# A layer with product-key experts: 170 gathered tokens, 1 MB weight loads, and output chunks held in PSUM

## The chip, the cores and the metric

One core of a Trainium2 chip runs the whole layer. The metric is the device time of one execution in microseconds (us); the time before is the median of three runs.

## The reference

The layer has an attention part (a latent attention and a stick-breaking attention, gated and merged) over 512 frames and 16 meta tokens, and then an expert part, which the change is about. Width D is 2048; there are 16,384 experts, each a row of `u` and a row of `v`. Each token picks 16 experts in each of 8 heads, so 128 experts with weights:

```
q = (xb @ w_q).reshape(PEER_BLOCK, PEER_HEADS, 2, PEER_HALF)
s = einsum('thcd,hcnd->thcn', q, sub_keys)
s1, i1 = top_k(s[:, :, 0], 16);  s2, i2 = top_k(s[:, :, 1], 16)
top_s, top_pos = top_k(all sums s1 + s2, 16);  idx = the pairs' expert numbers
g = softmax(top_s)
h = einsum('tkd,td->tk', u[idx], xb)
act = g * gelu(h)
out = einsum('tk,tkd->td', act, v[idx])
```

The residual is added and a final RMSNorm taken.

## The kernel before

**Two ways for the experts.** Tokens are split. The first `ND` = 352 are *dense*: every expert is computed for all of them by matmuls, and a matrix of gates that is zero outside a token's 128 experts picks what counts. The last 160 are *gathered*: only their chosen rows of `u` and `v` are loaded, by indirect DMAs that GpSimd (POOL) issues, and VectorE (DVE) multiplies and sums them. Of these, 128 tokens lie one to a partition, one expert of each per load (128 loads of 1 MB). The other `NB` = 32 have `RB` = 4 partitions each, so 32 loads serve them. That makes `NR` = 160 row loads of `u` and as many of `v`.

**Precision.** Each fp32 weight tile of 128 x 1024 is loaded (`wr`), rounded by ScalarE (ACT) into `wh`, and VectorE makes the remainder `wl` (line 208). The moving side is split the same way. `mm3` (lines 218 to 221) then issues three matmuls for each 128 x 128 block of weights. `wr` has four buffers of 0.5 MB; in stage V every fourth weight tile takes `wr`, `wh` and `wl` from a small pool of its own, which makes five. `wh` and `wl` have three buffers and that one.

**Stage U** (line 1171) loops over 128 blocks of 128 experts. Each block loads two half tiles of `ut`, runs 48 matmuls of 352 columns into one PSUM bank, takes Gelu into `hb` and writes it to `h_d` in DRAM. Between the halves it advances two generators, both by hand: `steps` (routing of the three dense tiles of 128 tokens, on VectorE) and `gate_steps` (one-hot matmuls at line 1033 that build the gates, two per token, written to `g_d`). The gathered rows are spread by `PACE`: a curve of rows done against block number. `OWN` says from which row on the buffers of the group loads are no longer lent to rows. `send` issues a row load and `row_step` works a row off on VectorE (lines 1126 and 1133).

**Stage V** (line 1242) loops over 32 groups of 512 experts. `hin` and `gin` bring a group's hidden values and gates in, `gated` multiplies them, `group_split` rounds them into `vah` and `val`. Eight weight tiles of `vb` (256 output columns each) follow, giving 16 output chunks of 128 features, each with 12 matmuls. `TURN` alternates the order of the tiles, so that the last three tiles of a group come first in the next and their six chunks stay in PSUM between the two (`held_ps`). Every other chunk is added to `acc` in SBUF after each group (line 1291). The residual `ht_d` is loaded in pieces in groups 3 to 18. In the last group the gathered tokens' sums are brought into place, `fin_add` squares and sums, and `fin_out` norms and writes.

**Order.** The language's scheduler orders each engine's instructions. Every queue is then worked off in that order: SP issues the weight, `hin` and `gin` loads, POOL the row loads, ACT the residual loads. The extra dependencies in the code (without a wait) keep the rows spread.

Of the kernel before, what the change touches and what calls it, by code (L numbers as in the profile page):

```python
# [37 lines left out]
NB = 32  # L38
RB = P // NB
ND = TA - NB  # L40
# [6 lines left out]
NG = NK // GRP  # L47
IN_SPLITS = (512, 512, 64, 1024, 1024, 1024, D, D)
# [59 lines left out]
def _layout(x, positions, meta_tokens, norm_mix_g, w_in, mla_q_norm_g, mla_w_uq, mla_kv_norm_g,  # L108
# [52 lines left out]
    ut = u.reshape(NK, NK, 2, 8, P).transpose(0, 2, 4, 3, 1).reshape(NK * 2, P, 1024)  # L161
    vb = v.reshape(NG, GRP, P, 8, 256).transpose(0, 3, 2, 1, 4).reshape(NG * 8, P, 1024)
# [20 lines left out]
def body(tc, nc, a, dbg=None):  # L183
# [10 lines left out]
    more = {"n": 0, "pool": None, "raw": False, "of": (4, (1,))}  # L194

    def wtile(src, eng=None, parts=False):
# [3 lines left out]
        raw = (w_ if more["raw"] else wp).tile([P, 1024], F32, name="wr", tag="wr",  # L200
                                               bufs=1 if extra and more["raw"] else 4)
        hi = w_.tile([P, 1024], F32R, name="wh", tag="wh")
        lo = w_.tile([P, 1024], F32R, name="wl", tag="wl")

        def load(s):
            SP.dma_start(raw[:, s], src[:, s])
            more["last"] = S.activation(hi[:, s], raw[:, s], AF.Copy)  # L207
            more["lo"] = (eng or V).tensor_sub(lo[:, s], raw[:, s], hi[:, s].bitcast(F32))  # L208

        if parts:  # L210
            return hi, lo, load
        load(slice(0, 1024))
        return hi, lo
# [36 lines left out]
    gwb_d = dp.tile([NB, P], F32, name="gwb_d")  # L250
    eob_d = dp.tile([NB, P], I32, name="eob_d")
# [3 lines left out]
    def rstd(out, ssq, n, dim, pool, tags=("rs_v", "rs_r", "rs_t")):  # L255
        w = n // (2 if n > 512 else 1)
        for c0 in range(0, n, w):
            ps = ps_tile()
            T.matmul(ps[:, :w], ones, ssq[:, c0:c0 + w], start=True, stop=True)
            v = pool.tile([P, 512], F32, name="rs_v", tag=tags[0])  # L260
            r0 = pool.tile([P, 512], F32, name="rs_r", tag=tags[1])
            t = pool.tile([P, 512], F32, name="rs_t", tag=tags[2])
# [518 lines left out]
    with tc.tile_pool(name="outp", bufs=2, side="right") as op:  # L781
        late = []

        def natural(m, gr):
            pt_ = ps_tile()
            for j, x_ in enumerate((xg, xgb)):
                T.transpose(pt_[:, j * P:(j + 1) * P], gr[:, j], ident)
                S.activation(x_[:, m * P:(m + 1) * P], pt_[:, j * P:(j + 1) * P], AF.Copy)

        for m in range(KC):  # L790
# [25 lines left out]
            V.tensor_scalar(gr[:, 1].rearrange("p (t r) -> p t r", r=RB),  # L816
# [15 lines left out]
    actb = rp.tile([P, NB], F32, name="actb")  # L832
    gwb = rp.tile([P, NB], F32, name="gwb")
    eob = rp.tile([P, NB], I32, name="eob")
# [20 lines left out]
    def spread_rows():  # L855
        b0 = ND - (NT - 1) * P
        SP.dma_start(eob_d, er[b0:])
        SP.dma_start(gwb_d, gw_all[b0:, NT - 1])
        SP.dma_start(eob, eob_d.rearrange("t (r k) -> (t r) k", r=RB))
        SP.dma_start(gwb, gwb_d.rearrange("t (r k) -> (t r) k", r=RB))  # L860

# [44 lines left out]
    with tc.tile_pool(name="score", bufs=2, side="left") as sp_, \  # L906
# [28 lines left out]
        for hc in range(16):  # L935
# [28 lines left out]
            if hc == 1:  # L964
                pt_ = ps_tile()
                rr = sp_.tile([P, 4, NK], F32, name="sc")[:, 0]
                V.tensor_copy(rr.rearrange("p (t r) -> p t r", r=RB), rh_[:, ND:TA, None].to_broadcast([P, NB, RB]))
                T.transpose(pt_[:, :P], rh_[:, TA:], ident)
                T.transpose(pt_[:, P:2 * P], rr, ident)
                V.tensor_copy(rcol, pt_[:, :1])  # L970
                V.tensor_copy(rcolb, pt_[:, P:P + 1])
            if hc:
                scores(*late.pop(0))
            if hc % 8 == 0:
                wr_ = wp.tile([P, 1024], F32, name="wr", tag="wr", bufs=4)
# [29 lines left out]
    def gates_of(ti):  # L1005
# [10 lines left out]
        for t0 in range(0, n + 4, 4):  # L1016
            if t0:
                p0 = t0 - 4
                oh_, wo_ = (spare[c][:, p0 // 4 % 2] for c in range(2))
                for t in range(4):  # L1020
# [3 lines left out]
            if t0 < n:  # L1024
                V.tensor_tensor(spare[0][:, t0 // 4 % 2], idx[:, :, t0:t0 + 4, None].to_broadcast([P, 2, 4, P]),
                                iota_b, ALU.is_equal)
            yield
            gate_out()
            if t0:
                ps = ps_tile()  # L1030
                for t in range(4):
                    for c in range(2):
                        T.matmul(ps[:, t * P:(t + 1) * P], oh_[:, 1, t], wo_[:, c, t], start=c == 0, stop=c == 1)
                banks.append((ps, ti * P + p0))
            yield

# [3 lines left out]
    def gate_out(hold=3):  # L1040

        for _ in range(min(2, len(banks))):
            if banks[0][1] % TB == 0 and len(banks) < hold:
                return
            ps, tok = banks.pop(0)
# [6 lines left out]
            for hf, half in enumerate(gb["now"]):  # L1052
                after_gelu(S.activation(half[:, :, o:o + 4].rearrange("p i t -> p t i"),
                                        ps.rearrange("p (t f i) -> p f t i", t=4, f=2)[:, hf], AF.Copy))
                if o + 4 == TB or tok + 4 == ND:
# [33 lines left out]
    NR = P + NB  # L1089
# [3 lines left out]
    NU = NR + 6  # L1093
    PACE = (2, 12, 123, NK - 0.5), (0, 7, 161, NU)
    OWN = 156
# [3 lines left out]
    def send():  # L1099
# [14 lines left out]
        idx = eo[:, k:k + 1] if k < P else eob[:, k - P:k - P + 1]  # L1114
        G.indirect_dma_start(out=row[:], out_offset=None, in_=a[src],  # L1115
# [4 lines left out]
    def row_step(mark, lead):  # L1120
# [3 lines left out]
        (src, k), row = todo[n], rows.pop(n)  # L1124
        if src == "u":
            ins = V.scalar_tensor_tensor(row, row, 1.0, xg if k < P else xgb, ALU.mult, ALU.mult,  # L1126
                                         accum_out=act[:, k:k + 1] if k < P else actb[:, k - P:k - P + 1])
        else:
            y, w = (yv, act[:, k:k + 1]) if k < P else (yvb, actb[:, k - P:k - P + 1])
            if k in (0, P):  # L1130
                ins = V.tensor_scalar(y, row, w, None, ALU.mult)
            else:
                ins = V.scalar_tensor_tensor(y, row, w, y, ALU.mult, ALU.add)  # L1133
# [5 lines left out]
        if src == "u" and k == NR - 1:  # L1139
            S.activation(actb, actb, AF.Gelu, scale=rcolb)  # L1140
            V.tensor_mul(actb, actb, gwb)
# [29 lines left out]
    for e in range(NK):  # L1171
# [7 lines left out]
        ps = ps_tile()  # L1179
        for hf in range(2):  # L1180
            wh, wl = wtile(a["ut"][2 * e + hf])
# [7 lines left out]
            for _ in range(1 + hf if e < 12 or e % 8 == 0 else hf):  # L1189
                next(steps, None)  # L1190
# [3 lines left out]
        if e == NK - 2:  # L1194
            gated(*held[0])
            ready = [vi.tile([P, D], F32R, name=x, tag=t)[:, :GRP * ND].rearrange("p (j t) -> p j t", t=ND)
                     for x, t in (("vah", "gin"), ("val", "hin"))]
            split(*ready, held.pop(0)[0])
# [10 lines left out]
    more["raw"], more["of"] = True, (4, (0,))  # L1209
# [3 lines left out]
    def group_split(i, eng):  # L1213
        ah, al = [vp.tile([P, GRP, ND], F32R, name=x) for x in ("vah", "val")]
        split(ah, al, held.pop(i)[0], eng)
        return ah, al
# [15 lines left out]
    def fin_out(t0, t1):  # L1232
        rstd(rf[:, t0:t1], ssf[:, t0:t1], t1 - t0, D, vp)
# [6 lines left out]
    TURN = ((0, 1, 2, 3, 4, 5, 6, 7), (5, 6, 7, 3, 4, 0, 1, 2))  # L1240
    held_ps, begun = {}, set()
    for i in range(NG):
        ah, al = ready
        for g in {0: (1,), 1: (2, 3)}.get(i, ()):
            group_in(g)
        if i == NG - 1:
            assert gs["done"] == len(todo)
            ln_exp(more["last"])
            ps = ps_tile()
            for c in range(KC):  # L1250
                T.matmul(ps[:, c * NB:(c + 1) * NB], yvb[:, c * P:(c + 1) * P], C("sel"), start=True, stop=True)  # L1251
            V.tensor_add(acc[:, :, ND:TA], acc[:, :, ND:TA], ps[:, :KC * NB].rearrange("p (c t) -> p c t", t=NB))
# [7 lines left out]

        for qi, q8 in enumerate(TURN[i % 2]):
            wh, wl = wtile(a["vb"][i * 8 + q8])
            if i + 1 < NG and qi == QM:
                gated(*held[i + 1])
            if qi == 0 and 0 <= i - 3 < KC:
                hres = vp.tile([P, ND], F32, name="hres", bufs=1)
                for dst, t in ((hres, slice(0, ND)), (acc[:, i - 3, ND:], slice(ND, SEQ))):
                    ld = S.dma_start(dst, ht_d[i - 3][:, t])
                    tc.add_manual_dep(ld.ins, more["last"].ins.name, NOSYNC, reason="keeps the loads spread")
            if qi == 6 and 0 <= i - 3 < KC:  # L1270
                V.tensor_add(acc[:, i - 3, :ND], acc[:, i - 3, :ND], hres)
            if i + 1 < NG and qi == QS:
                ready = group_split(i + 1, V)
                if i and i + 3 < NG:
                    group_in(i + 3)
            for dc in range(2):
                c = q8 * 2 + dc
                goes_on, stays = c in held_ps, i + 1 < NG and qi >= 5
                ps = held_ps.pop(c) if goes_on else ps_tile()
# [4 lines left out]
                if stays:  # L1284
                    held_ps[c] = ps
# [9 lines left out]
                if i == NG - 1:  # L1295
                    fin_add(c, 0, ND, qi + dc == 0)
                    if (qi, dc) == (2, 0):
                        fin_out(ND, SEQ)
# [20 lines left out]
```

## Time and profile before

| | |
|---|---|
| median of 3 runs | 3680.87 us (3677.76 to 3683.68) |
| the profiled execution | 3683.72 us, span 3681.5 us |
| TensorE busy | 3630.1 us, 99% |
| VectorE, ScalarE, GpSimd busy | 71%, 40%, 19% |
| moved by DMA | 868.28 MB |
| stage U, stage V | about 1569 to 2657 us, 2657 to 3664 us |

The profile's page gives the busy share of each engine over the span and in 40 equal slices (one digit, tenths). A window's row gives, for each engine, busy us and number of instructions, then the granted clock of TensorE, the share that the 16 DMA engines were busy, and GB/s. A group's row gives line, engine, operation, out<-in, count, busy us and mean ns, and the engine's idle time just before with what ended it. A wait's row has total us, times and the longest.

### The profile page before, as it was taken

What the parts mean: (1) busy time and instruction counts of PE and PEld (TensorE: products, weight loads), DVE (VectorE), ACT (ScalarE), POOL (GpSimd) and SP (SyncE); (2) the same over time, 40 slices, a digit from 0 to 9 for tenths busy, and PEclk for the clock granted to TensorE, in tenths of its full rate; (3) what the DMA queues carried; (4) which work ended last, traced back from release to release, by engine and by line L of the source; (5) the groups of instructions that cost most, each with busy time, mean ns of one, the idle gap of its engine ahead of it and who ended that gap; (6) DMA issues with size and microseconds to landing.
All of it is one profiled execution on the core that took longest, in us unless ns stands there. A gap on an engine that the chain in (4) does not pass through costs nothing. (4 is left out here: it accounts for less than half of the span.)

```text
span 3681.5 us, 53353 instructions
## 1 busy us (share of the span) xinstructions
PE 3630.1 (99%) x21159; PEld 3377.5 (92%) x21159; DVE 2623.8 (71%) x3499; ACT 1475.3 (40%) x2360; POOL 702.1 (19%) x499
## 2 busy tenths in 40 slices
PE   9999999999999999999999999999999999999997
PEld 8888888887788878899999999999999999999997
DVE  5533334335644567899979877777689999999896
ACT  4233233234533232235656666664333333333333
POOL 1000000000011221112222322332232322322220
PEclk9999999999999999999999999999999999999998
DMA  4322222221144442268898989999899999999982
GB/s 167 101 100 92 98 93 97 95 98 41 46 143 138 144 156 87 97 250 298 318 351 309 374 335 341 348 342 362 318 374 368 366 365 365 370 357 348 350 335 96
DMA packets 216538, 868.28 MB, mean 236 GB/s; under 512 B 24352, under 2 KB 49632, under 8 KB 175328
## 3 DMA queue, kind: packets, MB, share of 16 engines
q1 hardware_dynamic: 132896, 463.49, 35.4%
q0 software_dynamic: 53440, 361.52, 25.7%
q10 hardware_dynamic: 29952, 39.86, 3.0%
q8 instruction: 166, 2.72, 0.3%
q14 instruction: 84, 0.69, 0.1%
HBM read 801.83 MB, written 62.95 MB: 235 GB/s over the span
## 5 line engine op out<-in xcount | busy, mean ns | idle before, releaser
L207 ACT ACTIVATE wh<-wr 128x1024 fp32r<-128x1024 f32 (+1 forms) x756 | 789.1, 1054 | 1511.5 <-PE ps L221 1346.2
L208 DVE TENSOR_TENSOR wl<-wr,wh 128x1024 fp32r<-128x1024 f32 (+1 forms) x741 | 935.3, 1270 | 512.4 <-ACT wh L207 507.7
L219 PE MATMUL ps<-hgh,wl 128*128 128x352 f32 (+1 forms) x2304 | 773.2, 336 | 10.5 <-DVE wl L208 9.6
L221 PE MATMUL ps<-hgh,wh 128*128 128x352 f32 (+1 forms) x2304 | 768.3, 333 | 0.0
L220 PE MATMUL ps<-hgl,wh 128*128 128x352 f32 (+1 forms) x2304 | 765.1, 332 | 2.1 <-DVE hgl L225 2.0
L219 PE MATMUL ps<-vah,wl 128*128 128x352 f32 x2048 | 664.0, 324 | 4.1 <-DVE wl L208 3.9
L221 PE MATMUL ps<-vah,wh 128*128 128x352 f32 x2048 | 664.8, 325 | 0.0
L220 PE MATMUL ps<-val,wh 128*128 128x352 f32 x2048 | 661.0, 323 | 0.0
L219 PE MATMUL ps<-xh,wl 128*128 128x512 f32 (+1 forms) x1376 | 472.0, 343 | 6.0 <-ACT xh L312 6.0
L220 PE MATMUL ps<-xl,wh 128*128 128x512 f32 (+1 forms) x1376 | 470.1, 342 | 0.2 <-DVE xl L313 0.2
L221 PE MATMUL ps<-xh,wh 128*128 128x512 f32 (+1 forms) x1376 | 470.1, 342 | 0.0
L219 PEld LDWEIGHTS ps<-hgh,wl 128*128 128x128 f32 x2304 | 434.6, 189 | 25.0 <-DVE wl L208 11.9
L220 PEld LDWEIGHTS ps<-hgl,wh 128*128 128x128 f32 x2304 | 434.3, 189 | 14.5 <-DVE hgl L225 2.8
L221 PEld LDWEIGHTS ps<-hgh,wh 128*128 128x128 f32 x2304 | 433.5, 188 | 11.5 <-issue 0.2
L219 PEld LDWEIGHTS ps<-vah,wl 128*128 128x128 f32 x2048 | 386.2, 189 | 5.2 <-DVE wl L208 5.2
L221 PEld LDWEIGHTS ps<-vah,wh 128*128 128x128 f32 x2048 | 388.5, 190 | 0.0
L220 PEld LDWEIGHTS ps<-val,wh 128*128 128x128 f32 x2048 | 388.3, 190 | 0.0
L1115 POOL DMA_INDIRECT row<-v,eo x128 | 217.4, 1698 | 568.4 <-DVE xg L1133 522.7
L1133 DVE SCALAR_TENSOR_TENSOR xg<-row,act,xg 128x2048 f32<-128x2048 f32 x127 | 298.3, 2349 | 7.8 <-DMA row<-v,eo 7.8
L1115 POOL DMA_INDIRECT row<-u,eo x128 | 186.0, 1453 | 610.7 <-DVE row L1126 537.3
L219 PEld LDWEIGHTS ps<-xh,wl 128*128 128x128 f32 x1376 | 259.5, 189 | 37.8 <-ACT xh L312 6.4
L1126 DVE SCALAR_TENSOR_TENSOR row<-row,xg 128x2048 f32<-128x2048 f32 x128 | 292.5, 2285 | 0.5 <-DMA row<-u,eo 0.5
(453 smaller groups left out, 4744.8 us busy)
## 6 DMA issues: line engine op xcount, KB each, us to landing
wr<-ut SPq DMA_DIRECT2D x256, 512.0 KB, 6.3
wr<-vb SPq DMA_DIRECT2D x256, 512.0 KB, 6.7
wr<-front SPq DMA_DIRECT2D x238, 512.0 KB, 3.3
h_d<-hb ACTq DMA_DIRECT2D x128, 176.0 KB, 5.4
g_d<-gb POOLq DMA_DIRECT2D x44, 512.0 KB, 10.5
gin<-g_d SPq DMA_DIRECT2D x32, 704.0 KB, 5.8
hin<-h_d SPq DMA_DIRECT2D x32, 704.0 KB, 7.9
gates<-gt ACTq DMA_DIRECT2D x32, 256.0 KB, 2.0
```

The lines of the kernel that those rows point to most:

```text
L207: more["last"] = S.activation(hi[:, s], raw[:, s], AF.Copy)
L208: more["lo"] = (eng or V).tensor_sub(lo[:, s], raw[:, s], hi[:, s].bitcast(F32))
L219: T.matmul(ps, wl, xh, start=start, stop=False)
L220: T.matmul(ps, wh, xl, start=False, stop=False)
L221: T.matmul(ps, wh, xh, start=False, stop=stop)
L1115: G.indirect_dma_start(out=row[:], out_offset=None, in_=a[src], in_offset=bass.IndirectOffsetOnAxis(ap=idx, axis=0))
L1126: ins = V.scalar_tensor_tensor(row, row, 1.0, xg if k < P else xgb, ALU.mult, ALU.mult, accum_out=act[:, k:k + 1] if k < P else actb[:, k ...
L1133: ins = V.scalar_tensor_tensor(y, row, w, y, ALU.mult, ALU.add)
```

## The change

1. `NB` goes from 32 to 42, with `RB` = 3 partitions each: 170 tokens are gathered and `ND` = 342 are dense. The 42 tokens' 128 experts need `KB` = 43 loads of `PB` = 126 partitions (one slot is padded with index 0 and weight 0). The last gate step of a tile may have two tokens rather than four. `PACE`, `NU`, `OWN` and the number of routing steps per block are set anew.
2. `ut` and `vb` are laid out so that one DMA brings two half tiles, 1 MB with 8 KB per partition. `wr` becomes two buffers of 1 MB, also where the front stages load halves; stage V's own pool keeps `wh` and `wl` only.
3. Stage V's order: the four chunks of tiles 6 and 7 stay in PSUM for all 32 groups. Tiles 0 to 2 and 3 to 5 are taken in turn for two groups each (tile 0 of group 1, tile 0 of group 2, and so on), so that their chunks are added to `acc` after every second group. `vah` and `val` have three buffers. The residual of ten chunks is loaded straight into `acc`.

```
-NB = 32
+NB = 42
 RB = P // NB
+PB, KB = NB * RB, -(-P // RB)
 ND = TA - NB
+STAY = (6, 7)
+STEPS = [[(g, q) for q in ((0, 1, 2) if i % 2 == 0 else (3, 4, 5)) for g in (i - 1, i) if 0 <= g < NG] +
+         [(i, q) for q in STAY if i < NG] for i in range(NG + 1)]
...
+    def raw_pair(src):
+        t = wp.tile([P, 2048], F32, name="wr", tag="wr", bufs=2)
+        SP.dma_start(t, src)
+        return [t[:, :1024], t[:, 1024:]]
...
+        SP.dma_start(eob_d[:, P:], nil.bitcast(I32))
+        SP.dma_start(gwb_d[:, P:], nil)
...
-    NR = P + NB
+    NR = P + KB
-    NU = NR + 6
-    PACE = (2, 12, 123, NK - 0.5), (0, 7, 161, NU)
-    OWN = 156
+    NU = NR + 10
+    PACE = (2, 14, 124, NK - 0.5), (0, 10, 175.5, NU)
+    OWN = 172
...
-            wh, wl = wtile(a["ut"][2 * e + hf])
+            wh, wl = wtile(raw=raw[hf])
...
-            for _ in range(1 + hf if e < 12 or e % 8 == 0 else hf):
+            for _ in range(1 if e < 20 or e % 2 else hf):
                 next(steps, None)
...
-        for qi, q8 in enumerate(TURN[i % 2]):
-            wh, wl = wtile(a["vb"][i * 8 + q8])
+        for qi, (g, q8) in enumerate(step):
+            if at % 2 == 0:
+                pairs = raw_pair(a["vb"][at // 2])
+            wh, wl = wtile(raw=pairs[at % 2])
+            at += 1
...
+            if i == 0:
+                for c in (6, 7, 8, 9, 10, 11)[qi * 2:qi * 2 + 2]:
+                    residual(c, acc[:, c], slice(0, SEQ))
+            if qi == 0 and 9 <= i < 13:
+                residual(i + 3, acc[:, i + 3], slice(0, SEQ))
...
-                goes_on, stays = c in held_ps, i + 1 < NG and qi >= 5
+                goes_on = c in banks_of
+                stays = g < NG - 1 and (q8 in STAY or (g + 1, q8) in step)
...
-                    if (qi, dc) == (2, 0):
-                        fin_out(ND, SEQ)
+            if (i, qi) == (NG - 1, 2):
+                fin_out(ND, SEQ)
```

More of the change, by code (lines that the diff above doesn't have):

```diff
@@ L192, in ps_tile, with raw_half, wtile @@
         return pp.tile([P, 512], F32, name=name, tag="ps")
-    more = {"n": 0, "pool": None, "raw": False, "of": (4, (1,))}
-    def wtile(src, eng=None, parts=False):
+    more = {"n": 0, "pool": None, "of": (4, (1,)), "half": None}
+    def raw_half():
+        t, more["half"] = more["half"], None
+        if t is not None:
+            return t[:, 1024:]
+        more["half"] = wp.tile([P, 2048], F32, name="wr", tag="wr", bufs=2)
+        return more["half"][:, :1024]
+    def raw_pair(src):
+        t = wp.tile([P, 2048], F32, name="wr", tag="wr", bufs=2)
+        SP.dma_start(t, src)
+        return [t[:, :1024], t[:, 1024:]]
+    def wtile(src=None, eng=None, parts=False, raw=None):
         more["n"] += 1
@@ L199, in wtile @@
         w_ = more["pool"] if extra else wp
-        raw = (w_ if more["raw"] else wp).tile([P, 1024], F32, name="wr", tag="wr",
-                                               bufs=1 if extra and more["raw"] else 4)
+        there = raw is not None
+        raw = raw if there else raw_half()
         hi = w_.tile([P, 1024], F32R, name="wh", tag="wh")
@@ L205, in load @@
         def load(s):
-            SP.dma_start(raw[:, s], src[:, s])
+            if not there:
+                SP.dma_start(raw[:, s], src[:, s])
             more["last"] = S.activation(hi[:, s], raw[:, s], AF.Copy)
@@ L1019, in gates_of @@
                 oh_, wo_ = (spare[c][:, p0 // 4 % 2] for c in range(2))
-                for t in range(4):
+                for t in range(w_):
                     for c in range(2):
@@ L1030, in gates_of @@
                 ps = ps_tile()
-                for t in range(4):
+                for t in range(w_):
                     for c in range(2):
                         T.matmul(ps[:, t * P:(t + 1) * P], oh_[:, 1, t], wo_[:, c, t], start=c == 0, stop=c == 1)
-                banks.append((ps, ti * P + p0))
+                banks.append((ps, ti * P + p0, w_))
             yield
+            if w_ < 4:
+                break
     banks = []
@@ L1195, in body @@
             gated(*held[0])
-            ready = [vi.tile([P, D], F32R, name=x, tag=t)[:, :GRP * ND].rearrange("p (j t) -> p j t", t=ND)
-                     for x, t in (("vah", "gin"), ("val", "hin"))]
-            split(*ready, held.pop(0)[0])
+            parts = {0: [vi.tile([P, D], F32R, name=x, tag=t)[:, :GRP * ND].rearrange("p (j t) -> p j t", t=ND)
+                         for x, t in (("vah", "gin"), ("val", "hin"))]}
+            split(*parts[0], held.pop(0)[0])
         rows_due(e + 0.5)
@@ L1208, in body, with group_split @@
     vp = fin.enter_context(tc.tile_pool(name="vp", bufs=2, side="left", reuse_waits="tile"))
-    more["raw"], more["of"] = True, (4, (0,))
+    more["of"] = 4, (0,)
     more["pool"] = fin.enter_context(tc.tile_pool(name="weights_v", bufs=1, side="left", reuse_waits="tile"))
     acc = ap2.tile([P, KC, SEQ], F32, name="acc")
[L1213 to L1216, printed above, removed]
+    def group_split(g):
+        parts[g] = [vp.tile([P, GRP, ND], F32R, name=x, bufs=3) for x in ("vah", "val")]
+        split(*parts[g], held.pop(g)[0])
     n = 0
@@ L1238, in fin_out, with residual @@
             SP.dma_start(a["out"][c0:c0 + n, :, t0:t1].rearrange("k p t -> p k t"), acc[:, c0:c0 + n, t0:t1])
[L1240 to L1245, printed above, removed]
+    banks_of, begun, done, pairs = {}, {STAY[0] * 2 + c for c in range(4)} | set(range(6, 12)), [], []
+    def residual(c, dst, t):
+        ld = S.dma_start(dst, ht_d[c][:, t])
+        tc.add_manual_dep(ld.ins, more["last"].ins.name, NOSYNC, reason="keeps the loads spread")
+    at = 0
+    for i, step in enumerate(STEPS):
+        if i == 0:
+            group_in(1)
         if i == NG - 1:
@@ L1248, in body @@
             ln_exp(more["last"])
[L1249 to L1252, printed above, removed]
+            for c0 in range(0, KC, 8):
+                ps = ps_tile()
+                for c in range(c0, c0 + 8):
+                    T.matmul(ps[:, (c - c0) * NB:(c - c0 + 1) * NB], yvb[:PB, c * P:(c + 1) * P], C("sel")[:PB],
+                             start=True, stop=True)
+                V.tensor_add(acc[:, c0:c0 + 8, ND:TA], acc[:, c0:c0 + 8, ND:TA],
+                             ps[:, :8 * NB].rearrange("p (c t) -> p c t", t=NB))
             for c in range(0, KC, 4):
@@ L1259, in body @@
                     fin_add(c + j, ND, SEQ, c + j == 0)
-        for qi, q8 in enumerate(TURN[i % 2]):
-            wh, wl = wtile(a["vb"][i * 8 + q8])
+        for qi, (g, q8) in enumerate(step):
[3 more added lines that the diff above has]
+            at += 1
             if i + 1 < NG and qi == QM:
                 gated(*held[i + 1])
-            if qi == 0 and 0 <= i - 3 < KC:
+            if i == 0:
+                for c in (6, 7, 8, 9, 10, 11)[qi * 2:qi * 2 + 2]:
+                    residual(c, acc[:, c], slice(0, SEQ))
+            if qi == 0 and 3 <= i < 9:
                 hres = vp.tile([P, ND], F32, name="hres", bufs=1)
[L1267 to L1270, printed above, removed]
+                residual(i - 3, hres, slice(0, ND))
+                residual(i - 3, acc[:, i - 3, ND:], slice(ND, SEQ))
+            if qi == 0 and 9 <= i < 13:
+                residual(i + 3, acc[:, i + 3], slice(0, SEQ))
+            if qi == 6 and 3 <= i < 9:
                 V.tensor_add(acc[:, i - 3, :ND], acc[:, i - 3, :ND], hres)
[L1272 to L1275, printed above, removed]
+            if i + 1 < NG and qi == (QS if i else 4):
+                group_split(i + 1)
+                if i + 2 < NG:
+                    group_in(i + 2)
             for dc in range(2):
                 c = q8 * 2 + dc
-                goes_on, stays = c in held_ps, i + 1 < NG and qi >= 5
-                ps = held_ps.pop(c) if goes_on else ps_tile()
+                goes_on = c in banks_of
+                stays = g < NG - 1 and (q8 in STAY or (g + 1, q8) in step)
+                ps = banks_of.pop(c) if goes_on else ps_tile()
+                ah, al = parts[g]
                 for j in range(GRP):
@@ L1294, in body @@
                     row_step(mark, 3)
-                if i == NG - 1:
-                    fin_add(c, 0, ND, qi + dc == 0)
-                    if (qi, dc) == (2, 0):
-                        fin_out(ND, SEQ)
+                if i >= NG - 1 and not stays:
+                    fin_add(c, 0, ND, not done)
+                    done.append(c)
+            if (i, qi) == (NG - 1, 2):
+                fin_out(ND, SEQ)
+    assert sorted(done) == list(range(KC))
     fin_out(0, ND)
```

92 lines of the change are left out of this document (49 added, 43 removed).

## The prediction

> **What bounds the kernel now.** I read the page's shares and slices first, then the busy time by stage, then who waited for whom, then the groups and the transfers. Page, parts 1 and 2:
>
> ```profile
> PE 3630.1 (99%) x21159; PEld 3377.5 (92%) x21159; DVE 2623.8 (71%) x3499; ACT 1475.3 (40%) x2360; POOL 702.1 (19%) x499
> DVE  5533334335644567899979877777689999999896
> DMA  4322222221144442268898989999899999999982
> ```
>
> TensorE (PE) is busy 99% of the span and never leaves the path. But VectorE (DVE) and the transfers (DMA) stand at nines over the second half, the expert stages: a shorter TensorE there leans on both. Busy time by window, the window of 512-column matmuls first, then stages U and V:
>
> ```profile
> core 0: us, PE busy (x) PEld busy (x) DVE busy (x) ACT busy (x) POOL busy (x), PEclk, DMA share, GB/s
> 1040.00:1140.00 100.00, 100.00 (x429) 80.48 (x428) 48.04 (x45) 35.84 (x45) 11.61 (x9) 1.00 0.44 140
> 1695.00:1770.00 75.00, 70.78 (x447) 68.93 (x446) 74.21 (x111) 44.37 (x103) 18.09 (x14) 1.00 0.77 274
> 1770.00:1846.00 76.00, 72.07 (x452) 71.35 (x451) 71.34 (x102) 50.74 (x110) 21.66 (x16) 0.98 0.90 339
> 2120.00:2533.00 413.00, 413.00 (x2666) 412.98 (x2666) 313.76 (x277) 262.95 (x584) 127.78 (x93) 1.00 0.91 341
> 2657.00:2787.00 130.00, 126.05 (x769) 125.72 (x769) 115.83 (x103) 40.40 (x38) 38.28 (x22) 0.97 0.93 359
> 2787.00:3156.00 369.00, 368.88 (x2304) 368.38 (x2303) 342.36 (x314) 117.01 (x108) 103.34 (x62) 1.00 0.97 366
> 3156.00:3589.00 433.00, 433.00 (x2693) 432.71 (x2693) 394.73 (x355) 136.87 (x127) 114.72 (x70) 1.00 0.93 351
> ```
>
> From 1695 to 1846 VectorE is full and TensorE idles 8.1 us; after that TensorE idles only at V's start (4 us of 130) and the end. In V the DMA engines are at 0.97 with TensorE still full. The waits of TensorE say the same:
>
> ```profile
> PE ps L219 <- DVE wl L208: 13.6, 16, 3.9
> PE ps L259 <- DVE ssf L1230: 7.0, 2, 4.9
> ```
>
> **What a column costs.** A matmul's listed duration overlaps its neighbours, so I take the pitch. In V (2787 to 3156) every matmul has 352 columns: 369 us / 2304 = 160.2 ns. From 1040 to 1140 every one has 512: 100 / 429 = 233.1 ns. The slope is 72.9 / 160 = 0.456 ns a column. A third point, 264 columns, first and last of 21 starts in a row:
>
> ```profile
> 299.83 0.29 PE L219 MATMUL ps<-xh,wl 128*128 128x264 f32 x1
> 302.25 0.28 PE L221 MATMUL ps<-xh,wh 128*128 128x264 f32 x1
> ```
>
> 2.42 / 20 = 121 ns, against 160.2 - 88 x 0.456 = 120.1 by the line. So the pitch is proportional to columns from 264 to 512, and 342 lies inside: 155.6 ns.
>
> **The change part by part.** The matmuls concerned, and VectorE's work that comes and goes:
>
> ```profile
> L219 PE MATMUL ps<-hgh,wl 128*128 128x352 f32 x2048 | 670.8, 328 | 9.6 <-DVE wl L208 9.6
> L219 PE MATMUL ps<-vah,wl 128*128 128x352 f32 x2048 | 664.0, 324 | 4.1 <-DVE wl L208 3.9
> L1033 PE MATMUL ps<-hgl,hgh 128*128 128x128 f32 x704 | 88.3, 268 | 0.0
> L1126 DVE SCALAR_TENSOR_TENSOR row<-row,xg 128x2048 f32<-128x2048 f32 x128 | 292.5, 2285 | 0.5 <-DMA row<-u,eo 0.5
> L1126 DVE DVE_READ_ACCUMULATOR row<-row,xg 128x1 f32 x128 | 10.7, 84 | 0.0
> L1133 DVE SCALAR_TENSOR_TENSOR xg<-row,act,xg 128x2048 f32<-128x2048 f32 x127 | 298.3, 2349 | 7.8 <-DMA row<-v,eo 7.8
> L1291 DVE TENSOR_TENSOR acc<-acc,ps 128x352 f32<-128x352 f32 x310 | 157.8, 518 | 9.2 <-PE ps L221 9.2
> L207 ACT ACTIVATE wh<-wr 128x1024 fp32r<-128x1024 f32 (+1 forms) x756 | 789.1, 1054 | 1511.5 <-PE ps L221 1346.2
> L208 DVE TENSOR_TENSOR wl<-wr,wh 128x1024 fp32r<-128x1024 f32 (+1 forms) x741 | 935.3, 1270 | 512.4 <-ACT wh L207 507.7
> ```
>
> *Ten columns fewer (ND 352 to 342).* Lines 219 to 221, three products, run 2048 times in U and 2048 in V: 12,288 matmuls x 10 x 0.456 = **-56.0 us**, all on the path. [...]
>
> *Gate matmuls.* Two per dense token: 704 to 684. Eight of them and the next start, from stage U's timeline:
>
> ```profile
> 1992.66 1.00 PE L1033 MATMUL ps<-hgl,hgh 128*128 128x128 f32 x8
> 1993.50 0.38 PE L219 MATMUL ps<-hgh,wl 128*128 128x352 f32 x1
> ```
>
> 0.84 / 8 = 0.105 us each: 20 x 0.105 = **-2 us**.
>
> *22 more gathered rows.* The shared rows go from 128/4 to 43 loads of 126 partitions, so 171 u rows and 171 v rows instead of 160 each; U takes 181 of them (was 166), V 161 (was 154). VectorE pays 15 x 2.37 = +36 us in U (2285 ns and 84 ns for its accumulator) and 7 x 2.35 = +16 us in V. Neither is on TensorE's path while VectorE has room.
>
> *Room of VectorE in V.* Evictions: before, 10 of 16 chunks in a group are added to acc, afterwards 6 (four stay, the other twelve every second group). V's rows are spread over 484 of its 512 chunk passes. The window 2787 to 3156 holds 12 groups (2304 / 192), 192 passes: 48 x 0.518 = -25 us, and rows (161 - 154) x 192 / 484 = 2.8 x 2.35 = +7, so 342 becomes 324 of 358 us: 0.90 instead of 0.93. VectorE is relieved, cost 0; were that cover gone, each late half weight tile (1.3 us of wl) would stop TensorE directly.
>
> *Room of VectorE in U.* 2120 to 2533: rows go from (161-7)/(123-12) = 1.387 to (175.5-10)/(124-14) = 1.505 a block, over 48 blocks (48 x 48 of the 2666 matmuls) +5.6 rows: 314 + 13 = 327 of 402 us, free. The early stretch decides: the first routed tile's steps go at 2 a block over 18 blocks instead of 3 over 12. So the pile-up at 1695 to 1846 is thinned and the later one, at the third tile (about 1980), thickened by 1.5 against 1.25 steps a block. TensorE's loss of 8.1 us can go entirely, or double with 36 us more rows; I take **-4 us** (-8 to +8).
>
> *Transfers.* What 4 KB against 8 KB packets cost, page part 3 (q1 mostly weights in 4 KB packets, q0 mostly rows in 8 KB ones), and the times to land:
>
> ```profile
> q1 hardware_dynamic: 132896, 463.49, 35.4%
> q0 software_dynamic: 53440, 361.52, 25.7%
> wr<-ut SPq DMA_DIRECT2D x256, 512.0 KB, 6.3
> wr<-vb SPq DMA_DIRECT2D x256, 512.0 KB, 6.7
> hin<-h_d SPq DMA_DIRECT2D x32, 704.0 KB, 7.9
> row<-v,eo POOLq DMA_INDIRECT x128, 8.7
> ```
>
> Engine time per MB: q1 0.354 x 16 x 3681.5 / 463.5 = 45.0 us, q0 41.9. In 2787 to 3156 the engines work 0.97 x 369 = 358 us. Weights there are 96 x 0.524 = 50 MB; as 1 MB loads at q0's rate they save 50 x 3.1 / 16 = 10 us; rows add 2.9 MB, +8 us; hin is 3% smaller, -1. That makes 355 us of work in 358 us (2304 x 155.6): share 0.99. Without the saving by larger packets, 365: 1.02. So the cost is 0 to 7 us here, 0 to some 17 over V; below 0 is excluded, since no row shows TensorE losing to a load in this stretch. U in 2120 to 2533 comes to 376 + 15 - 10 = 381 of 402, 0.95: free. I take **+4 us** for V.
>
> *Two raw buffers of 1 MB in place of four of 0.5 MB (five in V).* A buffer is free only when both its halves are converted. Two pairs of TensorE work last 2 x 48 x 155.6 = 14.9 us; a buffer is held for landing (8.7 us, the 1 MB row being nearest) plus 2 x 1.05 of ACT and 1.3 of VectorE = 12.1 us. It fits with 2.8 us to spare: 0. In the front stages, where DMA is at 0.2 to 0.4 of the slices, likewise 0.
>
> *Four chunks in PSUM for all groups.* 4 + 2 in use + 2 being drained is 8 banks; a drain has two half tiles (7.5 us) for two adds of 0.5 us. No wait of TensorE for L1291 stands in its waits: 0, and at most one add (0.5 us) at a time if VectorE is late.
>
> *Start and end of V.* Four us idle at V's start are put down to wl, with PEclk at 0.97; the last pass has the 4.9 us on ssf. Residual loads are taken earlier and fewer adds stand before ssf, while three half tiles instead of two and a half lie ahead of that matmul: -2 us (+3 to -8). The 3 small DMAs and memset for padding the shared rows sit behind weight loads in SP's queue, under a us each: 0.
>
> **Sum.** The profiled execution took 3683.72 us for a span of 3681.5; the runs' median is 3680.87, 2.85 lower. 3683.7 - 56 - 2 - 4 + 4 - 2 = 3623.7; as a median of runs **3621 us**, 1.6% faster.
>
> **Rivals.**
> 1. *The buffer cycle binds: slower.* If 1 MB lands not in 8.7 but in twice the 0.5 MB time, 13.4 us, a cycle lasts 16.8 us, 1.9 over the two pairs. SP's queue is in order and in V also carries hin and gin, so I charge V's 128 pairs: 0.95 x 128 = +122 us: 3743 us. It decides from a mean landing of 11.5 us, and ends slower than before from about 12.5. For it: weights share the engines with rows throughout V. Against: the 6.7 us already contain waiting for the load ahead in the queue, and 1 MB rows land in 8.7. Chance 0.11.
> 2. *A ceiling on transfers.* The highest long row is 366 GB/s. V's first window would need (369 x 366 + 2700) / 358 = 384. If 366 is a ceiling whatever the packets, that window takes 376 us (+18), 2657 to 2787 some +6, 3156 to 3589 (152 MB and 3 of rows) 424 against 421 (+3): +27 in place of +4: 3644 us. [...] Chance 0.10.
> 3. *The pitch doesn't follow at 342 columns.* Then no 56 us: 3621 + 56 = 3677, no change that shows. [...] Against: the straight line through 264, 352 and 512. Chance 0.04.
>
> **How the numbers follow.** Forecast 0.75, rivals 0.11, 0.10 and 0.04. A measurement of this kernel can tell about 0.2% (7 us) from no change. Faster: 0.75 + 0.10 = 0.85; same 0.04; slower 0.11. The range: the low end has all unknowns well (3683.7 - 56 - 2 - 8 - 8 - 2.85 = 3607) and 3 us for the pitch's rounding, 3604; high end takes in the ceiling at 366 and some of its worse form: 3655. Left out are rivals 1 and 3 and half of rival 2's worse form, under 0.2.
>
> **What would show it.** Right: over 1280 matmuls per 200 us in V (155.6 ns); V's DMA share 0.97 to 1.00 at over 375 GB/s; 202 evictions of 512 chunk passes instead of 326; VectorE near 0.90 in V; 1 MB weights landing in 8 to 10 us; TensorE's idle for wl under 15 us. Wrong: landing over 12 us with TensorE waiting for wl all through V (rival 1); TensorE gaps with GB/s stuck at 366 (rival 2); 160 ns at 342 columns (rival 3); or TensorE losing more than 15 us around the routing of the second and third tile.

## The result and the profile after

The changed kernel takes **3829.5 us** (median of four runs, 3826.3 to 3852.3) beside 3680.0 for the kernel before: 1.042 times as long (95% interval 1.038 to 1.045). The prediction was 3621 us, range 3604 to 3655. Of the 209 us between forecast and result some 169 have one cause, which none of the rivals named: the 86 gathers of shared rows reach 126 partitions, not 128.

The execution in the profile took 3852.28 us, 23 more than the median, so what is read from it is a little too large. Page, parts 1 and 2 (shares of the DMA engines a little over 1, in rows further down, stand for full):

```profile
PE 3659.1 (95%) x21139; PEld 3391.0 (88%) x21139; DVE 2613.3 (68%) x3430; ACT 1451.9 (38%) x2336; POOL 705.8 (18%) x523
...
PE   9999999999999999999999999887899999998888
...
PEclk9999999999999999999999999888999999998989
DMA  4222222220344432688989999999989999999984
GB/s 160 99 99 102 89 98 99 88 88 34 102 138 141 142 112 97 228 317 319 346 325 356 365 366 311 255 257 269 344 349 351 366 380 368 371 345 279 269 265 143
```

TensorE falls below nine tenths in two places, the 26th to 29th slice and the last four. There the DMA engines are as busy as before, and move 255 to 279 GB/s (the edges, 344 and the end's 143, aside) where the slices between move 345 to 380. Engines that are full and move less: each byte costs more. The windows, first and third outside these two places, second and fourth inside:

```profile
core 0: us, PE busy (x) PEld busy (x) DVE busy (x) ACT busy (x) POOL busy (x), PEclk, DMA share, GB/s
2120.00:2320.00 200.00, 200.00 (x1337) 199.98 (x1336) 164.36 (x145) 134.18 (x300) 63.41 (x48) 1.00 0.98 366
2400.00:2700.00 300.00, 246.53 (x1366) 239.56 (x1365) 166.80 (x145) 110.79 (x222) 57.32 (x45) 0.87 1.01 263
2900.00:3380.00 480.00, 472.99 (x2988) 471.99 (x2987) 419.96 (x351) 148.45 (x141) 137.94 (x82) 0.99 0.96 368
3480.00:3740.00 260.00, 215.81 (x1250) 211.32 (x1249) 173.36 (x144) 59.59 (x58) 46.13 (x35) 0.91 0.95 269
```

At the first window's rate the second would hold 2005 matmuls; it holds 1366, which is 96 us lost in 300. By the third, the fourth would hold 1618 instead of 1250: 59 us in 260. TensorE is idle for 53 of these 96 us and 44 of these 59; the rest is lost while it is counted as busy, at a granted clock of 0.87 and 0.91. What the transfers cost there, queue by queue; first the window 2120 to 2320, then 2400 to 2700 (packets, MB, share of 16 engines):

```profile
q0 software_dynamic: 6851, 43.63, 58.0%
q1 hardware_dynamic: 3456, 25.17, 33.4%
...
q0 software_dynamic: 7258, 43.64, 55.5%
q1 hardware_dynamic: 4350, 30.35, 38.4%
...
row<-u,eob POOLq DMA_INDIRECT x33
```

Engine time per MB of the rows' queue is 0.580 x 16 x 200 / 43.63 = 42.5 us outside, as forecast, and 0.555 x 16 x 300 / 43.64 = 61.0 us inside. The weights' queue q1, whose loads did not change between the two windows, goes from 42.5 to 60.7 as well. So it isn't only that the shared rows are slow themselves: **while they are fetched, the weights beside them cost 1.4 times as much.** What distinguishes the window is the last line, the `eob` rows of 126 partitions; whether they are the cause is what e1 to e4 ask. In the end TensorE waits for weights (130.8 us for `wl`, 13.6 before) and ScalarE for raw ones:

```profile
PE ps L242 <- DVE wl L231: 130.8, 55, 10.2
PE ps L1062 <- ACT hgl L1051: 26.0, 18, 5.1
...
ACT wh L230 <- DMA wr<-vb: 579.6, 94, 18.5
ACT wh L230 <- DMA wr<-ut: 417.7, 95, 25.8
```

ScalarE waits for raw weights up to 25.8 us at a time; TensorE's weights are then late through `wh` and `wl`.

### The profile page after: what moved, and what is told of

The parts are those of the page before. It is cut to its first block, busy times and chain, and to the rows that moved or that the text cites. A ratio compares the mean times of both kernels' runs of the same rounds, so it can differ in the third digit from the quotient of the medians.

```text
span 3850.2 us, 52439 instructions
## 1 busy us (share of the span) xinstructions
PE 3659.1 (95%) x21139; PEld 3391.0 (88%) x21139; DVE 2613.3 (68%) x3430; ACT 1451.9 (38%) x2336; POOL 705.8 (18%) x523
## 4 chain that ended last, share of the span: by engine, by line
PE 47%; DMA 19%; DVE 15%; issue 14%; ACT 3%; POOL 2%; SPq 0%; ACTq 0%; DVEq 0%; POOLq 0%
PE ps L242 15%; PE ps L243 15%; PE ps L244 14%; DMA wr<-vb 6%; DMA wr<-ut 5%; DMA row<-v,eo 5%; DVE wl L231 5%; DVE xg L1163 3%; DVE row L1159 2%; ACT wh L230 1%; POOL row L1147 1%; DMA row<-u,eob 1%; DMA hin<-h_d 1%; DVE hgh L1054 1%; DVE xgb L1163 1%
## 5 line engine op out<-in xcount | busy, mean ns | idle before, releaser
L242 PE MATMUL ps<-hgh,wl 128*128 128x342 f32 (+1 forms) x2304 | 777.4, 337 | 58.5 <-DVE wl L231 55.9
L243 PE MATMUL ps<-hgl,wh 128*128 128x342 f32 (+1 forms) x2304 | 773.3, 336 | 0.9 <-DVE hgl L248 0.9
L244 PE MATMUL ps<-hgh,wh 128*128 128x342 f32 (+1 forms) x2304 | 767.3, 333 | 0.0
L242 PE MATMUL ps<-vah,wl 128*128 128x342 f32 x2048 | 670.7, 328 | 74.9 <-DVE wl L231 74.8
L243 PE MATMUL ps<-val,wh 128*128 128x342 f32 x2048 | 665.1, 325 | 0.0
L244 PE MATMUL ps<-vah,wh 128*128 128x342 f32 x2048 | 663.0, 324 | 0.0
L242 PEld LDWEIGHTS ps<-hgh,wl 128*128 128x128 f32 x2304 | 448.9, 195 | 78.5 <-DVE wl L231 62.2
L243 PEld LDWEIGHTS ps<-hgl,wh 128*128 128x128 f32 x2304 | 447.9, 194 | 11.4 <-DVE hgl L248 1.9
L244 PEld LDWEIGHTS ps<-hgh,wh 128*128 128x128 f32 x2304 | 447.0, 194 | 10.9 <-issue 0.2
L243 PEld LDWEIGHTS ps<-xl,wh 128*128 128x128 f32 x1376 | 259.2, 188 | 32.0 <-DVE xl L336 1.3
```

The costliest lines, as they stand in the source:

```text
L242: T.matmul(ps, wl, xh, start=start, stop=False)
L243: T.matmul(ps, wh, xl, start=False, stop=False)
L244: T.matmul(ps, wh, xh, start=False, stop=stop)
```

## The experiments

**Theory A: the 126 partitions.** Theory A says that these gathers slow all transfers. Against it stands B, that the cycle of the two 1 MB buffers binds.

*e1: the changed kernel, shared rows fetched for all 128 partitions.* The two more partitions get index 0; nothing reads them.

```
+        V.memset(eob, 0)
...
-        row = row[:P if k < P else PB]
-        idx = eo[:, k:k + 1] if k < P else eob[:PB, k - P:k - P + 1]
+        idx = eo[:, k:k + 1] if k < P else eob[:, k - P:k - P + 1]
```

> The changed kernel, with the 86 shared row loads (43 of u, 43 of v) gathering 128 partitions instead of 126; the two extra partitions fetch row 0 and nothing reads them. In the changed kernel's trace the time is lost in two stretches, 2320 to 2750 us and 3450 to 3765 us, where these loads run: 430 us there for work worth 320 at the 342-column pitch, and 315 for 242, so 183 us. Theory A (a gather of 126 partitions slows the whole transfer system): the loss goes, 3829 - 183 = about 3646 us, GB/s in both stretches back over 340 and the 8 KB packets back from 0.50 to 0.31 us. Theory B (the cycle of two 1 MB buffers binds): nothing changes, 3820 to 3835 us.

Measured: 3660.3 us, 0.9946 (0.9930 to 0.9963) of the kernel before. Fetching *more* bytes takes 169 us off (A had 183), or 169 / 86 = 2.0 us a load. The stretch of this run in which 27 `eob` rows are fetched:

```profile
2330.00:2480.00 150.00, 150.00 (x1006) 150.00 (x1005) 123.00 (x110) 106.76 (x242) 48.33 (x35) 1.00 0.97 367
```

TensorE is full beside the `eob` rows, at 367 GB/s.

*e2, e3, e4: the kernel before, with its 64 shared loads cut to 126, 112 and 120 partitions.* This asks for the converse, and which property of the number matters. These three kernels leave out 2, 16 and 8 of the shared tokens' expert slots, and the steps that use these rows are cut to the same partitions.

```
+        if k >= P:
+            row, idx = row[:126], idx[:126]
...
```

> The kernel before with one thing altered: its 64 shared row loads gather 126 partitions instead of 128 (two expert slots of the last shared token are left out). Loads of 0.5 MB, four buffers and the old order of stage V stay. Theory A: 64 loads at the 183 / 86 = 2.1 us that each such load cost in the changed kernel, 3680 + 136 = about 3816 us, less if four buffers hide a part (over 3750). Theory B: 3680 us as before.

> The kernel before with its 64 shared row loads gathering 112 partitions (16 expert slots of the shared tokens are left out). [...] Theory B: 3680 us.

> The kernel before, with its 64 loads of shared rows taken for 120 partitions (the last eight slots of the shared rows are left out). [...]

Measured: 3784.4 us (1.029, 1.027 to 1.031), 3740.0 us (1.017, 1.015 to 1.019) and 3805.7 us (1.034, 1.032 to 1.036). That is 1.7, 1.0 and 2.0 us for each of the 64 loads, in a kernel that has nothing else of the change; B, which had no loss, falls. The window 2450 to 2600 before and with 120 partitions:

```profile
2450.00:2600.00 150.00, 150.00 (x947) 150.00 (x946) 112.27 (x99) 70.41 (x125) 39.77 (x28) 1.00 0.95 362
```

```profile
2450.00:2600.00 150.00, 133.26 (x762) 128.75 (x760) 82.85 (x73) 60.65 (x116) 31.89 (x24) 0.93 1.03 277
```

And the median times to land in it, before and with 126 partitions:

```profile
wr<-ut SPq DMA_DIRECT2D x37, 512.0 KB, 7.7
...
row<-u,eob POOLq DMA_INDIRECT x23, 9.8
```

```profile
wr<-ut SPq DMA_DIRECT2D x28, 512.0 KB, 16.1
...
row<-u,eob POOLq DMA_INDIRECT x20, 21.8
```

The weights, 128 partitions as ever, land in twice the time. Of the three counts only 112 divides by 16, the number of DMA engines: it loses least, 1.0 us a load, but it loses; 120 loses most.

*e10: all 128 partitions again, but each shared load in two gathers of 64.*

```
...
+        SP.dma_start(eob2[:64], eob_d.rearrange("t (r k) -> (t r) k", r=RB)[64:])
...
-        G.indirect_dma_start(out=row[:], out_offset=None, in_=a[src],
-                             in_offset=bass.IndirectOffsetOnAxis(ap=idx, axis=0))
+        for dst, ix in ([(row[:], idx)] if k < P else [(row[:64], idx[:64]), (row[64:], eob2[:64, k - P:k - P + 1])]):
+            G.indirect_dma_start(out=dst, out_offset=None, in_=a[src],
+                                 in_offset=bass.IndirectOffsetOnAxis(ap=ix, axis=0))
```

> The kernel before, with each of its 64 shared row loads issued as two gathers of 64 partitions. [...]

Measured: 3802.6 us, 1.035 (1.031 to 1.038), 1.9 us for each pair, with the same bytes to the same places.

```profile
2450.00:2600.00 150.00, 132.22 (x748) 127.37 (x747) 84.45 (x73) 59.62 (x115) 55.52 (x48) 0.92 1.03 275
```

So it is neither the bytes nor a rest in a division by 16. This run also issues twice as many gathers, which no run tells apart from their size; e2 to e4 don't. Of the five counts tried (64, 112, 120, 126, 128) only the gather to all 128 partitions leaves the weights beside it their speed. Their queue in the window 2450 to 2600, before, then with 112, 126, 120 and twice 64 partitions:

```profile
q1 hardware_dynamic: 6093, 23.15, 41.7%
q1 hardware_dynamic: 4917, 18.50, 41.2%
q1 hardware_dynamic: 4039, 14.79, 35.0%
q1 hardware_dynamic: 4056, 14.79, 35.8%
q1 hardware_dynamic: 3990, 14.51, 36.4%
```

By share x 16 x 150 / MB that is 43.2 us of engine time per MB before, then 53.4, 56.8, 58.1 and 60.2. Why the weights pay too was not shown: no trace here says which engine carries what.

**Where the rest went.** e1 is 39 us above the forecast. The next runs all fetch 128 partitions.

*e5: e1 with the weights in 0.5 MB loads and four buffers.*

```
-        t = wp.tile([P, 2048], F32, name="wr", tag="wr", bufs=2)
-        SP.dma_start(t, src)
-        return [t[:, :1024], t[:, 1024:]]
+        return [src[:, :1024], src[:, 1024:]]
...
```

with one load and one of four buffers for each half in `wtile`.

> The changed kernel with the shared rows fetched for 128 partitions (3660 us, some 39 above the forecast), and its weight loads put back to 0.5 MB in four buffers. Theory B1 (the larger loads relieve the DMA engines in stage V, as the forecast has it): without them V's transfer share passes 1.0 and it loses 5 to 20 us: 3665 to 3680 us. Theory B2 (a 1 MB buffer is held until both its halves are converted, and this is what makes TensorE wait at the pile-ups of stage U and at the border to V): 20 to 35 us better, 3625 to 3640 us.

Measured: 3646.4 us, 14 less than e1: B2 in kind, though it had 20 to 35. ScalarE's waits from 1620 to 2100 us, the pile-ups of stage U, in e1:

```profile
ACT wh L230 <- DMA wr<-ut: 158.2, 48, 8.5
```

and in e5:

```profile
ACT wh L223 <- DMA wr<-ut: 16.7, 8, 3.1
```

With two large buffers ScalarE stands waiting for weights; with four small ones it has them. TensorE's idle time in these 480 us is 480 - 458.72 = 21.3 us in e1 and 480 - 468.60 = 11.4 in e5:

```profile
1620.00:2100.00 480.00, 458.72 (x2942) 452.33 (x2941) 446.84 (x631) 272.44 (x571) 127.84 (x99) 0.99 0.91 329
```

```profile
1620.00:2100.00 480.00, 468.60 (x3053) 464.55 (x3052) 458.15 (x627) 285.09 (x595) 131.76 (x104) 1.00 0.93 343
```

Yet the large loads land in 7.8 and 7.5 us over the run (6.6 in this stretch), faster than the 8.7 assumed:

```profile
wr<-ut SPq DMA_DIRECT2D x128, 1024.0 KB, 7.8
wr<-vb SPq DMA_DIRECT2D x128, 1024.0 KB, 7.5
```

It is the hold that grew, not the landing: the next load can't start until VectorE has made the second half's remainder, and in the pile-ups VectorE is late. In the changed kernel, with the same loads, SyncE, which issues them, waits in this stretch 46 times for a `wl`, 349.6 us in all or 7.6 on average, and VectorE is busy 447.16 of the 480 us.

*e6: e1 with the routing steps at the old pace.* (`1 + hf if e < 12 or e % 8 == 0 else hf` steps per half block.)

> The changed kernel with the shared rows fetched for 128 partitions, and the routing steps of stage U at the pace of the kernel before (three a block for the first twelve blocks, then one). Theory C1 (the 38 us over the pitch between 1700 and 2100 us come from the thinner pace of the routing, which puts the first two tiles beside more rows): 15 to 25 us better, 3635 to 3645 us. Theory C2 (they come from the 22 more row loads and their VectorE work in stage U): within 8 us of 3660. Theory C3 (the thinner pace does help, as forecast, by 4 to 8 us): 3664 to 3670 us.

Measured: 3661.6 us. The pace of the routing does nothing either way; C2.

*e7: e1 with 32 shared tokens,* so that the large loads and V's order are all that is left of the change.

```
-NB = 42
+NB = 32
...
```

with the pace of rows and routing of the kernel before.

> The changed kernel with 32 shared tokens instead of 42 (352 columns, 160 row loads, all of 128 partitions, pace of rows and routing as before): only the 1 MB loads and the order of stage V are left of the change. Theory D1 (these two parts cost TensorE nothing and gain nothing while it is 99% busy): 3670 to 3682 us. Theory D2 (they bring waits of their own at the start of V and in U's pile-ups, which is where the forecast's missing 39 us went): 3690 to 3715 us.

Measured: 3705.7 us, 1.007 (1.005 to 1.009). These two parts cost 28 us and bring nothing: D2.

*e8: part 1 alone,* 170 tokens, with the loads and V's order of the kernel before.

> Only the first part of the change: 170 gathered tokens (the shared rows fetched for 128 partitions), with the 0.5 MB loads and the order of stage V of the kernel before. By the forecast's columns alone 3678 - 58 = 3620 us. Theory E1 (the new order of stage V costs some 25 us, as the run with 352 columns suggests once its large loads' 14 us are taken off): this is faster than the version with 0.5 MB loads and the new order (3646): 3620 to 3636 us. Theory E2 (what is lost is the price of 11 more row loads in each stage, VectorE and DMA at 0.97 and more, and the new order relieves it): 3646 us or more, up to 3665.

Measured: **3633.8 us, 0.9876 (0.9850 to 0.9903)**, the best version tried; it beats both kernels: E1. Against e5 (3646.4) the new order costs 12.6 us. In this difference stands one thing more: e8 has stage V's fifth 0.5 MB buffer again, which e5 lacks, and no run tells it apart from the order. With the large loads' 13.9 that makes 26.5, and e7 had 28 for both: the parts add up. Where the order costs, from 2540 to 2900 us, e8 and then e5:

```profile
2540.00:2900.00 360.00, 349.69 (x2187) 347.14 (x2186) 315.31 (x283) 112.79 (x113) 93.41 (x59) 0.99 0.96 367
```

```profile
2540.00:2900.00 360.00, 335.05 (x2071) 331.11 (x2070) 285.97 (x239) 107.29 (x108) 93.23 (x55) 0.98 0.94 358
```

116 matmuls fewer, 18 us at 157 ns. At the end the new order gives 6 back. TensorE waits for `ssf`, the sum of squares for the last norm, 7.7 us in e8 and 1.7 in e5:

```profile
PE ps L267 <- DVE ssf L1245: 7.7, 2, 5.7
```

```profile
PE ps L275 <- DVE ssf L1253: 1.7, 1, 1.7
```

*Four attempts at those 18 us.* e9 is e5 and loads the residual of chunks 6 to 11 later, one a step:

> The version with 128-partition shared rows and 0.5 MB loads in the new order (3646 us), with the residual of chunks 6 to 11 no longer loaded in the first step of stage V (six loads of 256 KB among hidden values, gates and weights) but one chunk a step from the fourth on, as chunks 0 to 5 are. Theory F1 (these 1.5 MB are what crowds the border between U and V, where this version loses some 29 us against the pitch): 8 to 20 us better, 3626 to 3638 us. Theory F2 (the border is crowded by the group loads and the rows moved up into U): within 5 us of 3646.

Measured: 3643.7 us, 3 less: F2. e11 is e5 with hidden values and gates loaded two groups ahead (`group_in(i + 3)` for `group_in(i + 2)`):

> The version with 128-partition shared rows and 0.5 MB loads in the new order (3646 us), with each group's hidden values and gates loaded two groups ahead of their use, as the kernel before does, instead of one. Theory G1 (in the new order VectorE waits for these loads, six times and 23 us between 2550 and 2900 us where the old order has one wait of 6 us, and the weight remainders behind it come late; that is most of the new order's 12 us): 5 to 12 us better, 3634 to 3641 us. Theory G2 (the loads are late because the DMA engines are full there, however early they are issued): within 4 us of 3646, or slower.

Measured: 3648.9 us: no gain, G2. e12 is e11 with six of the ten v rows moved back from U into V (`NU = NR + 4`):

> The run before this one, with four v rows instead of ten fetched in stage U and a thinner pace of rows before its end (stage V takes 167 instead of 161; VectorE is busy 56 to 60 us of every 60 there in the new order). Theory H1 (the 8 to 12 us that the last blocks of U lose come from the rows moved into them): another 5 to 10 us better, 3627 to 3635 us. Theory H2 (those blocks lose to the first group's loads, or V then loses as much): within 4 us of the run before, or slower.

Measured: 3650.2 us: no gain, H2. e13 is e9 with all eight tiles of group 0 in the first step, so that group 1 is needed after eight tiles, not five:

```
+STEPS[0][3:3] = [(0, 3), (0, 4), (0, 5)]
+STEPS[1] = [b for b in STEPS[1] if b[0]]
...
```

> The new order with 128-partition shared rows, 0.5 MB loads and the late residual (3644 us), with all eight tiles of group 0 in the first step, as in the kernel before; the second step then has five tiles of group 1. Group 1's hidden values and gates are so needed after eight tiles instead of five, some 23 us later. Theory I1 (the new order's 12 us are lost because group 1 is needed three tiles sooner, while the last of U is still being written and the rows moved into U are fetched): 6 to 12 us better, 3632 to 3638 us, and the 17 us over the pitch in its first two groups fall under 8. Theory I2 (it is not this; rows and weights are late there in any order): within 4 us of 3644.

Measured: 3638.6 us (3635.5 to 3639.4), 5 less than e9 (3640.7 to 3648.0), where 6 to 12 were expected under I1. Beside the kernel before, the 95% intervals of e13 (0.9874 to 0.9907) and e9 (0.9882 to 0.9933) overlap, so the size is rough. The window 2540 to 2900 in e9, then e13:

```profile
2540.00:2900.00 360.00, 339.91 (x2091) 337.55 (x2090) 290.10 (x242) 110.96 (x111) 89.28 (x56) 0.97 0.93 357
```

```profile
2540.00:2900.00 360.00, 344.25 (x2139) 342.08 (x2138) 298.06 (x252) 111.99 (x112) 98.68 (x58) 0.98 0.95 364
```

48 matmuls more, 7.5 us. The sooner need of group 1 is, by this, part of the order's price; what is left between this version and e8, 4.8 us, is not found.

## Why the prediction was wrong

**The step that failed** is "22 more gathered rows", together with "Transfers". The prediction named the "43 loads of 126 partitions" and then priced them, and everything beside them, by rows of loads to 128: the 41.9 us of engine time per MB from the queue's total. No row of the trace before had a gather to fewer partitions. A cost without a row of its own should have been bounded from both sides; this one was taken as known. The 126-partition form costs 1.7 us a load in the kernel before and 2.0 in this one, 169 us in all, and its measure is 61 us per MB on both queues. Without it (e1) the kernel is 3660 us: faster by 0.5%, still 5 us above the range.

The other steps, by what the runs show:

- *Ten columns: right.* In U, 55 us hold 342 matmuls before and 355 in e8; in V, 600 us hold 3735 and 3817. Before, then e8:

```profile
2535.00:2590.00 55.00, 55.00 (x342) 55.00 (x341) 39.15 (x34) 18.46 (x22) 8.44 (x6) 1.00 0.95 373
2900.00:3500.00 600.00, 599.88 (x3735) 599.30 (x3734) 548.81 (x495) 190.01 (x175) 165.53 (x100) 1.00 0.95 359
```

```profile
2496.00:2551.00 55.00, 55.00 (x355) 55.00 (x354) 41.08 (x36) 16.66 (x20) 16.75 (x13) 1.00 1.02 418
...
2900.00:3500.00 600.00, 599.83 (x3817) 599.55 (x3816) 572.97 (x536) 193.15 (x180) 169.09 (x106) 1.00 0.98 377
```

  160.8 to 154.9 ns and 160.6 to 157.2 ns: (5.9 + 3.4) ns x 6144 = 57 us for 56.0 forecast, though not shared evenly between the stages. e8 as a whole is 46.6 us faster than the kernel before, 12 short of columns and gate matmuls together. Some 6 of these are more idle time of TensorE in the window with V's start: 10.3 us in e8's row above, 4.0 before. The rest is not found.

```profile
2540.00:2900.00 360.00, 356.05 (x2197) 355.51 (x2196) 299.63 (x266) 114.64 (x118) 90.78 (x54) 0.99 0.94 358
```

- *Transfers in V: +4, near in size by luck.* With the large loads (e1) TensorE is idle 3.7 us of the same 600. But this comes with the large loads, which the sum had as a saving: e5, in the same order with small ones, is idle 0.3 us at share 0.97, e8 0.2 at 0.98, where the sum without the saving had 1.02 and up to 17 us. The 45.0 us per MB for 4 KB packets was an average over the whole run. In V before, weights cost 0.469 x 16 x 200 / 35.55 = 42.2 and rows 42.3, so there was hardly anything to save:

```profile
q1 hardware_dynamic: 9080, 35.55, 46.9%
q0 software_dynamic: 4836, 35.28, 46.6%
```

  These are of the window 2900 to 3100 before; the row of e5:

```profile
2900.00:3500.00 600.00, 599.71 (x3817) 599.43 (x3816) 534.20 (x442) 193.53 (x179) 176.04 (x106) 1.00 0.97 371
```

  Rival 2 falls with e8's row: 377 GB/s held over 600 us, above the "ceiling" of 366, and 418 over 55. No run shows the "worse form" of it that the high end of the range, 3655 us, took in.
- *VectorE's room in V: right.* It would have 0.90; e1 has 530.51 of 600, 0.88 (row below). e8 does without the relief at 572.97, 0.95, and TensorE stays full: four chunks in PSUM bought nothing here.

```profile
2900.00:3500.00 600.00, 596.28 (x3784) 594.22 (x3783) 530.51 (x442) 187.41 (x178) 168.62 (x106) 1.00 0.96 371
```

- *Two raw buffers: 0, mis-sized by 14 us* (10 of them in U's pile-ups, 3.4 in V, by the idle times above). The cycle was worked out for a stretch where TensorE sets the pace (12.1 of 14.9 us) and carried over to U's pile-ups, where VectorE does and holds the buffer longer. Rival 1 had the mechanism (the buffer cycle) in the wrong place, by the wrong cause: it looked at the landing and at V.
- *U early: -4, no sign of it.* TensorE is idle 480 - 470.37 = 9.6 us from 1620 to 2100 before, 11.4 in e5. The routing's pace, on which the step rested, moves nothing (e6).

```profile
1620.00:2100.00 480.00, 470.37 (x2987) 467.33 (x2986) 439.83 (x615) 286.26 (x604) 122.95 (x94) 1.00 0.87 322
```

- *Start and end of V: -2, mis-sized by some 14 us.* The end gained 6, inside the +3 to -8; the start lost 18, which was costed at nothing. That the new order needs group 1 after five tiles instead of eight stood in the diff and was not priced; it is, roughly, 5 to 8 us (e13).

What the prediction asked to be looked at did tell: TensorE's idle for `wl` is 130.8 us where under 15 was "right", with GB/s stuck, though not at 366 but at 263 and only beside `eob` rows. Here the rate fell from 366 to 263 GB/s while the DMA engines stayed full (0.98, then 1.01), and that pointed to the cost of each byte.

**Left open:** why 112 partitions cost half of what 120 do, and through what a gather slows the queue beside it; some 5 of the 12.6 us between e5 and e8, with the part that the fifth buffer has in them; and some 6 of the 12 us that e8 falls short.

## What to carry to other kernels

A gather's number of partitions was a form of its own here (1.0 to 2.0 us more a load below 128): price it only by rows of the same form, and if there are none, bound it, above all when the DMA engines are as busy as in these windows (0.95 and more) and the weights beside it pay. Filling unused partitions with a dummy index was worth 169 us here though it moves more bytes. And a change with three parts is worth costing as three: here one brought 47 us, and the other two lost 27. They brought nothing because what they relieve (VectorE in V, the cost of small packets) wasn't short, and lost by a longer hold of the buffers and by the new order's start.

## What the runs showed of the hardware

- Gathers of 8 KB rows to 64, 112, 120 or 126 partitions lowered the rate of all queues together to between 263 and 293 GB/s at a busy share of 0.95 to 1.03; in the windows set beside them, with gathers to 128 partitions, it was 362 to 368 at 0.95 to 0.98. The window with 112 partitions:

```profile
2450.00:2600.00 150.00, 135.00 (x823) 133.55 (x823) 92.87 (x81) 62.67 (x113) 30.73 (x25) 0.95 1.00 293
```

- One core sustained 377 GB/s over 600 us beside a full TensorE, and 418 GB/s over 55 us.
- In stage V of the kernel before, a MB cost the DMA engines the same on the weights' queue, mostly 4 KB packets, as on the rows', mostly 8 KB ones: 42.2 and 42.3 us.
- The pitch of 342-column matmuls was 154.9 ns in U and 157.2 in V, where 352 columns had 160.8 and 160.6: the same form, with operands in other tiles.
